# Segment mean over sorted ids: the in-kernel list planner gets measured fetch latencies, real sizes of the table work, and planned constants

## The chip, the cores and the metric

One core of one Trainium2 chip. The metric is device time in microseconds (us), the median of several executions of the one program. Engine names in the profile: DVE is VectorE, ACT is ScalarE, POOL is GpSimd, SP is SyncE, PE is TensorE.

## The reference, cut to what matters

```python
n, num_segments = 10_000_000, 10000
data        = np.random.randn(n).astype(np.float32)
segment_ids = np.sort(np.random.randint(0, num_segments, n))

sums, counts = np.zeros(num_segments, np.float32), np.zeros(num_segments, np.float32)
np.add.at(sums, segment_ids, data)
np.add.at(counts, segment_ids, 1)
return sums / np.maximum(counts, 1)
```

The ids are sorted, and a segment has about 1000 elements. The kernel never loads all ids. It lays the data out as 128 partitions by 78125 elements and cuts each partition into 90 rows of 875. A row holds at most one boundary between two segments. It finds the place of that boundary (the **cut** of the row) from a few probed ids and one short gathered run of ids.

## The kernel before

Each row costs VectorE one `split` (the sum left of the cut; rows, splits and cuts are counted from 0) and ScalarE one `total`. A cut needs a chain over four engines: SyncE loads probes, VectorE turns them into an index, GpSimd issues a gather of 175 or 208 ids for each partition, ScalarE sums the gathered ids, and VectorE makes the cut from the sum. 90 gathers share a ring of 18 buffers.

```python
def gather(odd, r, i):                                  # GpSimd
    n, idx = (WO, IDXO) if odd else (W, IDX)
    nc.gpsimd.indirect_dma_start(out=GT[:, i % RING, 0:n], ...,
        in_offset=bass.IndirectOffsetOnAxis(ap=idx[:, r : r + 1], axis=0), ...)

def add_ids(odd, r, i):                                 # ScalarE
    nc.scalar.activation(out=junk_a[:, 0:n], in_=gt32[:, i % RING, 0 : 2 * n : 2],
        func=ACT.Copy, accum_out=to[:, r : r + 1])

def split(r):                                           # VectorE, 90 times
    nc.vector.scalar_tensor_tensor(
        out=junk_v[:, 0:n], in0=iota[:, 0:n], scalar=KK[:, r : r + 1], in1=d,
        op0=ALU.is_lt, op1=ALU.mult, accum_out=A[:, r : r + 1])
```

All splits write their unused product into one buffer, `junk_v`. ScalarE does the same: every `total` and every `add_ids` writes into `junk_a`.

Nothing is scheduled at run time. While the program is built, a small simulation (class `Plan`) decides in which order each engine gets its instructions. Its idea of time is a handful of numbers:

```python
free = {"V": 4.0, "A": 6.2, "P": 3.0, "S": 0.75}        # when each engine starts
...
if moves:                                               # a load or a gather
    pipes[e].append([n, moves, now + 1.2])              # start-up, then moving
...
if pipes[e][0][1] <= 0:                                 # moved: when is it seen?
    heapq.heappush(events, (now + 1.25, len(out), pipes[e].popleft()[0]))
```

Table work (counts, prefix sums, tables of segments, checks) is tied to splits by hand: `put(r, steps, every)` hangs one or more steps behind split `r`, then behind split `r + 1`, and so on.

## Time and profile before

| | before |
|---|---|
| time | 215.02 us, median of 3 (214.88 to 215.25) |
| span of the profiled run | 212.3 us |
| busy: DVE, ACT, POOL | 142.7, 138.2, 99.6 us |
| split | 90 times, 1116 ns each |
| gather on POOL | 90 times, 1.0 us each, one per 1.3 us at best |

The lines of this profile are shown in the prediction below. No engine is busy all the time, and VectorE, the busiest, idles some 70 us. The question is what each hole of VectorE waits for.

### The profile page before, as it was taken

How to read it: one execution, taken by the hardware profiler on the slowest of the kernel's cores; microseconds unless marked ns; L12 is line 12 of the kernel's file. 1: busy time of each engine (PE TensorE's matmuls, PEld its weight loads, DVE VectorE, ACT ScalarE, POOL GpSimd, SP SyncE). 2: the span in 40 equal slices, each digit the busy share in tenths (PEclk: the TensorE clock that was granted, in tenths of full speed). 3: DMA queues.
4: the chain of work that ended last, by engine and by line, in shares of the span. 5: the costliest groups of instructions: out<-in, count | busy, mean ns of one | idle time of the engine just before them, and what ended most of it. 6: DMA issues, size and time to landing. Idle time of an engine off the chain costs nothing.

```text
span 212.3 us, 1523 instructions
## 1 busy us (share of the span) xinstructions
PE 1.6 (1%) x6; PEld 1.4 (1%) x6; DVE 142.7 (67%) x501; ACT 138.2 (65%) x362; POOL 99.6 (47%) x121
## 2 busy tenths in 40 slices
PE   0000000000000010000000000000000000010000
PEld 0000000000000010000000000000000000000000
DVE  6425083849904945974391789937927999987992
ACT  8429256546358478936883982878768997669700
POOL 5561756514773777377357147720730002883000
DMA  5999999999999999999999999999993000330000
GB/s 83 281 275 225 273 255 285 278 299 347 364 342 359 350 361 356 346 402 407 403 407 380 318 320 406 400 403 418 416 399 131 0 0 3 87 96 0 0 2 11
DMA packets 49782, 55.67 MB, mean 262 GB/s; under 512 B 39633, under 2 KB 40201, under 8 KB 49768
## 3 DMA queue, kind: packets, MB, share of 16 engines
q1 hardware_dynamic: 43835, 40.33, 59.0%
q0 software_dynamic: 5760, 15.22, 21.2%
q14 instruction: 15, 0.11, 0.2%
q10 hardware_dynamic: 172, 0.00, 0.1%
HBM read 57.81 MB, written 0.04 MB: 272 GB/s over the span
## 4 chain that ended last, share of the span: by engine, by line
issue 25%; DMA 22%; SPq 21%; DVE 15%; POOL 8%; ACT 5%; POOLq 0%; ACTq 0%; DVEq 0%
SPq L237 14%; DMA GT<-in_segment_ids_dram,IDXO 10%; POOL GT L412 8%; DVE junk_v L513 8%; DMA GT<-in_segment_ids_dram,IDX 8%; SPq L252 7%; DMA data_t<-in_data_dram 4%; ACT junk_a L508 3%; ACT junk_a L423 2%; POOLq L412 0%; DVE shf L859 0%; DVE most L932 0%; DVE pa L888 0%; DVE add L924 0%; POOL pb L890 0%
## 5 line engine op out<-in xcount | busy, mean ns | idle before, releaser
L513 DVE SCALAR_TENSOR_TENSOR junk_v<-iota,q,data_t 128x875 bf16<-128x875 f32 x90 | 100.5, 1116 | 0.8
L508 ACT ACTIVATE junk_a<-data_t 128x875 bf16<-128x875 f32 x90 | 83.6, 929 | 4.6 <-DVE FE L385 1.8
L412 POOL DMA_INDIRECT GT<-in_segment_ids_dram,IDX x49 | 49.3, 1007 | 51.6 <-DVE IDX L394 22.8
L423 ACT ACTIVATE junk_a<-GT 128x175 bf16<-128x175 int32 (+1 forms) x90 | 33.4, 372 | 56.8 <-DMA GT<-in_segment_ids_dram,IDX 32.5
L412 POOL DMA_INDIRECT GT<-in_segment_ids_dram,IDXO x41 | 41.1, 1002 | 39.1 <-DVE SR L488 14.6
L433 DVE SCALAR_TENSOR_TENSOR q<-YY,GS 128x6 f32<-128x6 f32 (+1 forms) x9 | 1.5, 166 | 34.2 <-ACT junk_a L423 34.2
L508 ACT ACTIVATION_READ_ACCUMULATOR junk_a<-data_t 128x1 f32 x90 | 16.8, 187 | 0.0
L423 ACT ACTIVATION_READ_ACCUMULATOR junk_a<-GT 128x1 f32 x90 | 16.8, 186 | 0.0
L500 DVE TENSOR_TENSOR q<-YO,GSO 128x3 f32<-128x3 f32 (+1 forms) x14 | 2.2, 160 | 21.4 <-ACT junk_a L423 21.3
L513 DVE DVE_READ_ACCUMULATOR junk_v<-iota,q,data_t 128x1 f32 x90 | 7.3, 82 | 0.0
L268 ACT ACTIVATE GT<-q 128x3744 int32<-128x3744 f32 x1 | 3.5, 3533 | 0.0
L369 DVE CAST VV<-pr 128x12 f32<-128x12 int32 (+1 forms) x9 | 1.5, 165 | 2.9 <-DMA pr<-in_segment_ids_dram 2.9
L924 POOL TENSOR_TENSOR xa<-pa,RG 128x528 f32<-128x528 f32 x1 | 1.2, 1247 | 3.6 <-DVE ps L746 3.6
L326 DVE CAST jj<-jj_i 128x128 f32<-128x128 int32 x1 | 1.5, 1485 | 0.7 <-POOL jj_i L325 0.7
L491 DVE SCALAR_TENSOR_TENSOR YO<-VV,SR 128x6 f32<-128x6 f32 (+2 forms) x9 | 1.8, 201 | 0.2
L385 DVE TENSOR_SCALAR FE<-ST 128x6 f32<-128x6 f32 (+2 forms) x10 | 1.9, 194 | 0.0
L268 ACT ACT_TABLE_LOAD x1 | 1.3, 1283 | 0.7 <-PEq L1130 0.7
L390 DVE TENSOR_TENSOR ST<-ST,FE 128x6 f32<-128x6 f32 (+2 forms) x10 | 1.6, 163 | 0.1
L394 DVE SCALAR_TENSOR_TENSOR IDX<-ST,wb 128x6 int32<-128x6 f32 (+2 forms) x11 | 1.7, 161 | 0.0
L399 DVE SCALAR_TENSOR_TENSOR YY<-ST,SG 128x6 f32<-128x6 f32 (+2 forms) x10 | 1.7, 168 | 0.0
L891 POOL TENSOR_SCALAR pb<-pb 128x168 f32<-128x168 f32 (+1 forms) x2 | 1.6, 787 | 0.2
L439 DVE TENSOR_SCALAR q<-q 128x6 f32<-128x6 f32 (+1 forms) x9 | 1.5, 169 | 0.2
(151 smaller groups left out, 61.5 us busy)
## 6 DMA issues: line engine op xcount, KB each, us to landing
data_t<-in_data_dram SPq DMA_DIRECT2D x44, 875.0 KB, 13.2
GT<-in_segment_ids_dram,IDX POOLq DMA_INDIRECT x49, 6.5
pr<-in_segment_ids_dram SPq DMA_DIRECT2D x42, 6.0 KB, 6.2
GT<-in_segment_ids_dram,IDXO POOLq DMA_INDIRECT x41, 6.8
data_t<-in_data_dram SPq DMA_DIRECT2D x1, 437.5 KB, 14.8
data_t<-in_data_dram SPq DMA_DIRECT2D x1, 125.0 KB, 14.7
out_dram<-OUT SPq DMA_DIRECT2D x1, 36.6 KB, 2.6
pt<-in_segment_ids_dram SPq DMA_DIRECT2D x2, 11.0 KB, 7.4
```

The costliest lines, as they stand in the source:

```text
L237: nc.sync.dma_start(out=pr[:, a:b, :], in_=bass.AP(ids_p.tensor, ids_p.offset + 2 * L * a, [list(ids_p.ap[0]), [2 * L, b - a], [S, K + 1]]),)
L252: nc.sync.dma_start(out=d[:, 0 : c - a], in_=data_p[:, a:c])
L268: nc.scalar.activation(out=gt32[:, :, 0 : 2 * WO : 2], in_=view(q5[:, 0, 0:1], [[0, RING], [0, WO]]), func=ACT.Copy)
L385: v.tensor_scalar(out=FE[:, a:b], in0=ST[:, a:b], scalar1=0.0, scalar2=FAR, op0=ALU.is_equal, op1=ALU.mult)
L394: v.scalar_tensor_tensor(out=IDX[:, c:d], in0=ST[:, c:d], scalar=float(w), in1=wb[:, c:d], op0=ALU.mult, op1=ALU.add)
L399: v.scalar_tensor_tensor(out=YY[:, a:b], in0=ST[:, a:b], scalar=float(K + 1), in1=SG[:, a:b], op0=ALU.mult, op1=ALU.add)
L412: nc.gpsimd.indirect_dma_start(out=GT[:, i % RING, 0:n], out_offset=None, in_=ids2d[:], in_offset=bass.IndirectOffsetOnAxis(ap=idx[:, r : ...
L423: nc.scalar.activation(out=junk_a[:, 0:n], in_=gt32[:, i % RING, 0 : 2 * n : 2], func=ACT.Copy, accum_out=to[:, r : r + 1],)
L491: nc.vector.scalar_tensor_tensor(out=YO[:, c:d], in0=VV[:, 2 * c + 1 : 2 * d : 2], scalar=float(WO), in1=SR[:, c:d], op0=ALU.mult, op1=ALU ...
L500: nc.vector.tensor_sub(out=KK[:, 2 * c + 1 : 2 * d : 2], in0=YO[:, c:d], in1=GSO[:, c:d])
L508: nc.scalar.activation(out=junk_a[:, 0:n], in_=d, func=ACT.Copy, accum_out=t)
L513: nc.vector.scalar_tensor_tensor(out=junk_v[:, 0:n], in0=iota[:, 0:n], scalar=KK[:, r : r + 1], in1=d, op0=ALU.is_lt, op1=ALU.mult, accum_ ...
```

## The change

The intent: let the planner know what a fetch really takes, so that it stops placing cuts too early; give it the true sizes of table steps and let it place them itself against deadlines; and take constants out of the start.

```diff
-        free = {"V": 4.0, "A": 6.2, "P": 3.0, "S": 0.75}
+        free = {"V": 3.4, "A": 6.2, "P": 2.2, "S": 0.75}
...
-                    heapq.heappush(events, (now + 1.25, len(out), pipes[e].popleft()[0]))
+                    heapq.heappush(events, (now + (1.4 if e == "S" else 3.8), len(out), pipes[e].popleft()[0]))
...
-    def put(r, steps, every=1, needs=()):
-        for i, f in enumerate(steps):
-            after[r + i // every].append((f, needs))
+    def put(name, by, steps, needs=(), past=()):
+        deps = list(needs) + [ends[n] for n in past or ("copy",)]
+        for i, f in enumerate(steps):
+            busy = getattr(f, "busy", 0.1)
+            plan.add((name, i), "V", busy, deps, by, f, late=busy + 0.1)
+            deps = [(name, i)]
+        ends[name] = deps[0]
...
-    put(E + 1, extend(), needs=cut_of_rows(E) + totals(E))
-    put(E + 6, ext_rows())
-    put(37, keys(0, 48), needs=[("E", 6, 0)])
+    put("ext", 40, extend() + ext_rows(), cuts(E) + rows(E) + seen(E))
+    put("keys0", 44, keys(0, 48), seen(48))
... (some 25 more such sequences)
-    nc.gpsimd.iota(rp_i[:, 0:NR], ...)                 # and 28 more constants, at once
+    for n, f in enumerate(ramps):
+        plan.add(("ramp", n), "P", 0.25, [], 5.5, f)
+    for n, f in enumerate(copies):
+        small(("copy", n), [...], 2.2, f)
... (probes of later rows asked for 27 instead of 31 rows ahead; the last seven rows' ids
     loaded row by row; one rule of the choice between split and small work, and 0.1 us more for a split right
     after a split)
```

## The prediction

> **What bounds the kernel now.** I read the view of cores first (one core, span 212.3 us, clock 1.000, so no throttling), then the busy slices of the page, the stretches of the span with each engine's busy time, the waits, and the order in time of VectorE (DVE) and GpSimd (POOL) around the long waits. The slices come first, because they show when the transfers stop:
>
> ```profile
> DVE  6425083849904945974391789937927999987992
> ACT  8429256546358478936883982878768997669700
> POOL 5561756514773777377357147720730002883000
> DMA  5999999999999999999999999999993000330000
> ```
>
> A slice is 5.3 us. The DMA row is full from the second slice to the 30th and then falls, so the bulk of the data has been fetched by about 163 us. DVE is the other way round: full of holes before that point, and nearly solid after it. The stretches put numbers on it (width, then busy time of PE, PEld, DVE, ACT, POOL with counts, clock, DMA share, GB/s):
>
> ```profile
> 18.78:60.00 41.22, 0.00 (x0) 0.00 (x0) 27.16 (x109) 20.97 (x64) 22.80 (x23) 1.00 1.08 287
> 60.00:107.00 47.00, 0.98 (x4) 0.93 (x4) 26.13 (x88) 34.09 (x103) 29.08 (x30) 1.00 1.05 372
> 107.00:163.40 56.40, 0.00 (x0) 0.00 (x0) 39.40 (x129) 41.15 (x113) 26.11 (x26) 1.00 0.99 370
> 163.40:208.30 44.90, 0.59 (x2) 0.50 (x2) 42.51 (x133) 31.26 (x70) 12.21 (x15) 1.00 0.08 22
> ```
>
> While data arrives DVE idles 14.1, 20.9 and 17.0 us; afterwards it works off 45 us of backlog with 2.4 us idle. The end is therefore set by DVE: 142.7 us of its own work, plus its holes, plus 4.0 us for the output. The view of waits names the holes:
>
> ```profile
> DVE q L433 <- ACT junk_a L423: 34.2, 9, 7.3
> DVE q L500 <- ACT junk_a L423: 21.3, 6, 5.6
> DVE VV L369 <- DMA pr<-in_segment_ids_dram: 2.9, 1, 2.9
> DVE q L449 <- ACT junk_a L423: 1.9, 2, 1.2
> ```
>
> L433, L500 and L449 turn sums of gathered ids into the cut position of a row. 57.4 us go to them: DVE reached the cut before its gathers had landed and been summed by ACT, and because its program is one fixed order, rows that were ready behind the cut stood still. The timeline of DVE shows the longest such place. This cut's six indices were written at 49.10, but on POOL its last gather started only at 59.15, behind others; DVE has nothing placed before the cut but index work that ends at 58.8:
>
> ```profile
> 58.56 0.17 DVE L394 SCALAR_TENSOR_TENSOR IDX<-ST,wb 128x6 int32<-128x6 f32 x1
> 66.05 0.17 DVE L433 SCALAR_TENSOR_TENSOR q<-YY,GS 128x6 f32<-128x6 f32 x1 [7.25 <-ACT junk_a L423]
> ```
>
> The DMA issues say why: a gather needs 6.5 to 6.8 us from issue to landing, while the planner of before counts 1.2 us to start, 0.40 or 0.47 us of moving, and 1.25 us to land.
>
> ```profile
> GT<-in_segment_ids_dram,IDX POOLq DMA_INDIRECT x49, 6.5
> GT<-in_segment_ids_dram,IDXO POOLq DMA_INDIRECT x41, 6.8
> ```
>
> **What the Trainium skill says.** "PSUM — Partial Sum Buffer", Engine vs sequencer instructions: ScalarE, VectorE and GpSimd queues are strictly first in, first out. The 7.25 us hole agrees. "Perfetto Trace Analysis", DMA Instruction — SWDGE (GPSIMD): the profiled end of a gather is the end of descriptor writing, not of the movement. It agrees: POOL shows 1.00 us per gather, issue to landing is 6.5. "DMA: Bandwidth & Descriptors", Anatomy of one DMA — SWDGE (gpsimd) path: 2.0 us fixed plus bytes at 436 GB/s. A gather of 128x175 ids of 8 bytes is 179 KB, so 2.4 us as an estimate from that page; the trace has 3.0 us only for the last seven gathers, issued after the data had stopped, and 5 to 8.5 us under load, so the measured time is what I use.
>
> **The change, part by part.** No arithmetic is dropped; the change re-sorts the same work. (1) The planner's landing time of a gather goes from 1.25 to 3.8 us (with 1.2 and 0.4: 5.4 us plus sharing), of a data or probe load to 1.4. In the built program the order moves accordingly. In before, the gathers of even and odd cuts alternate on POOL, and an odd one not yet computable holds up the even ones behind it: POOL stood still 14.6 us on SR and 8.9 us on IDXO. In after, all three even gathers of the second group go ahead of the first odd one. On DVE, the first six-row even cut (the one of the 7.25 us) has 12 splits, 5 to 16, between its indices and itself, where before it had 6; the next such cut has 11. (2) The table work becomes sequences with real sizes and a deadline; the sizes of the instructions stay. (3) Fourteen constants leave DVE's start-up and fill holes; ident's fill moves to POOL. (4) The last seven rows' ids are fetched row by row, and their indices come before split 69, where before they came before split 72; in before POOL sat idle 22.8 us and then cost DVE only 1.9 us, so this is small.
>
> Value of (3): DVE's first probe work waits for its fetch at 6.7 us either way, and the first cut needs gathers issued at 8.7, 10.2 and 11.5 plus about 5.7 us landing and 0.6 us of ACT, thus 18 us in both. The 2 us of constants fall into holes: 0 to 0.5 us at the end. The gain must come from (1).
>
> **Working of the new waits.** I walk the new order with durations of the old trace: 1.17 us from split to split (49.88, 51.05, 52.23 in the timeline), 0.08 to 0.12 us for a small operation, the listed duration for bigger ones, 1.3 us from gather to gather on POOL (1.00 busy, 0.30 gap), landing 5.5 us up to 45 us, 6.6 up to 90, 7.3 later and 8.2 near 140 (what the gathers of before took in those stretches), and 0.6 us for ACT's sum and the signal. Each cut starts at the later of DVE reaching it and its last gather being summed. The start-up idle up to the first split stays at 11 us. From there:
> - First odd cut: its two gathers can be issued at 20.3 and 21.6, ready 27.7; DVE has nothing else and waits 4.8. The next three cuts wait 0.3, 1.6, 0.9.
> - Split 16 ends at 52 us (before: 56.8). The fourth odd cut: gathers 47.0 to 49.6, ready 56.9, reached 53.5: 3.4.
> - Up to split 28 the cuts have slack: the fifth even group is ready at 73 and reached at 75.
> - From 77 to 98 us POOL runs without gap, and the cuts follow its beat: waits of 0.7, 1.2, 1.5, 1.9 and 3.2 us (the last for six gathers ending at 98.3, ready 106.3, reached 103.1). Split 44 ends near 108; in before it is near 127.
> - After that 0.3, 1.2, 2.5 and 1.3 us, and about 0.8 us for the matmul behind the verdict, which now has little work beside it. Split 77 ends near 163.5.
> These are 25.6 us; with the 11 at the start, the 2.5 us that before has beyond its named waits (65.6 idle to 208.3, 63.1 named), and perhaps 1 us for the last total, 40 us of idle. DVE's end is 142.7 + 40 = 183; the output adds 4.0, the span is 187. The measured median of before is 2.7 us over its profiled span (215.0 against 212.3), so the time is 189 to 190; I take **189 us**, 12% less.
>
> Data does not stop this: the transfers have the same bytes and end near 160. Split 77 needs the 39th of 45 tiles; at a pace of some 2.2 us a tile that lands near 149, and it is used at 163. The ring of 18 tiles also stops blocking: at split 44 near 108 us, 40 tiles may be issued.
>
> **The rivals.** *Floor by transfers.* If the waits vanish more fully than in my walk, the last tile decides: landing at 160 to 163, two splits, and 5 us to the end, plus some 5 us of table work after split 87. That gives a span of 172 and a time of 175. For it: DMA was full all along; against: POOL's 90 gathers at 1.3 us are 117 us by themselves, and the first odd cuts chain two gathers one after the other. *Latency grows with the load.* In before the sync queue stood blocked for a free tile (one load 15.25 us in the DMA queue's timeline), which thinned the traffic. A faster DVE frees tiles sooner, so gathers would meet a full queue from 60 us on: 8.2 instead of 7 us each, seen at 130 to 150 us. Some ten tight cuts by about 1 us: 199. *A fixed order with a wrong model still waits.* Only positions moved, and ACT is in order too: a sum of ids behind a total whose tile is late holds a cut. If half of the 57 us survive at other cuts, the time is 200 to 205. *Nothing gained*, since the holes only move to the tail: against it stands that the tail is solid work on DVE, so every earlier split shortens it.
>
> **Range and chances.** The walk gives 189; about 175 is the floor; latency under load gives up to 199. I put 80% on 180 to 199. For a gain under 2% (above 210.7) more than 50 of the 57 us would have to return; slower needs new waits. Chances: faster 0.97, same 0.02, slower 0.01.
>
> **What would show it right or wrong.** Right: DVE busy stays within 1.5 us of 142.7; waits of DVE on ACT's id sums fall from 57 us to between 22 and 32; DMA still ends near 160; split 44 ends near 108, and the stretch after the data stops shrinks from 45 to about 21 us, still solid. The start to the first split stays near 19 us. Wrong on the first step, if DVE's waits stay above 40 us; on the floor, if DVE begins to wait for data tiles near the end; on the latency, if gathers have a median above 8 us; on the constants, if the first split comes before 17 us.

## The result, and the profile after

The changed kernel took **200.89 us** (median of 4, 200.19 to 202.13), the kernel before in the same rounds 215.13 us. The ratio is 0.9345, 95% interval 0.9296 to 0.9395. Ratios here are the mean time of one kernel's runs over that of the other's runs of the same rounds, so they are not quite the ratio of the quoted medians. Executions over 1.5% slower than the fastest of the same kernel are left out of the means. It is a gain of 6.5% where 12% was predicted: right in direction, 12 us short, and just outside the range.

The slices of the page, as in the prediction, now 5.0 us each:

```profile
DVE  6225475549939851599559717989979978999990
POOL 8537777751457777017777401767406958402000
DMA  5999999999999999999999999999999824200000
```

DVE is fuller from the middle on, but thin slices remain at 35 to 45 us (8th and 9th) and at 70 to 85 us (15th to 17th). The stretches, in the columns of the prediction:

```profile
18.78:60.00 41.22, 0.00 (x0) 0.00 (x0) 24.67 (x92) 25.13 (x77) 24.65 (x25) 1.00 1.10 302
60.00:107.00 47.00, 0.99 (x4) 0.93 (x4) 33.08 (x123) 31.08 (x89) 29.18 (x30) 1.00 1.06 358
107.00:163.40 56.40, 0.00 (x0) 0.00 (x0) 45.07 (x137) 44.71 (x116) 27.32 (x30) 1.00 0.98 372
163.40:197.00 33.60, 0.58 (x2) 0.50 (x2) 31.18 (x92) 24.57 (x60) 8.30 (x8) 1.00 0.12 31
```

DVE's work before 163.4 us grew, and the backlog after it shrank from 45 to about 33 us; the prediction had 21. The first stretch (18.78 to 60) got worse: 16.6 us idle instead of 14.1. The view of waits of the changed kernel, its longest rows (total, times, longest; "..." marks a row left out):

```profile
DVE VV L389 <- DMA pr<-in_segment_ids_dram: 12.4, 4, 5.6
DVE q L520 <- ACT junk_a L443: 8.1, 6, 3.3
DVE q L453 <- ACT junk_a L443: 6.6, 2, 5.3
DVE junk_v L533 <- remote: 5.8, 3, 2.5
DVE q L520 <- issue: 4.7, 4, 2.0
DVE PX L818 <- issue: 3.7, 1, 3.7
...
DVE junk_v L533 <- issue: 1.7, 1, 1.7
```

The cuts (L453 and L520) now wait 19.4 us where they waited 57: this part worked even better than predicted. But other rows grew. VectorE waits for probes (L389) for 14.5 us (this row and one of 2.1 us that is left out), where it was 2.9 before; some 9 us of this lie before the first split, which starts at 17.3 us, not later than the 18.8 of before. And, which is new, it waits before splits (L533) and table steps (L818) for "remote" or "issue", that is, for nothing that the profile can name. Its timeline shows what these are. Before splits:

```profile
36.94 1.13 DVE L533 SCALAR_TENSOR_TENSOR junk_v<-iota,q,data_t 128x875 bf16<-128x875 f32 x1 [0.76 <-DVE YY L419]
...
39.76 1.13 DVE L533 SCALAR_TENSOR_TENSOR junk_v<-iota,q,data_t 128x875 bf16<-128x875 f32 x1 [1.68 <-remote]
...
42.59 1.13 DVE L533 SCALAR_TENSOR_TENSOR junk_v<-iota,q,data_t 128x875 bf16<-128x875 f32 x1 [1.70 <-issue]
```

and before table steps:

```profile
77.12 0.18 DVE L653 TENSOR_TENSOR delta<-sp,base 128x1 f32<-128x1 f32 x1
81.01 0.26 DVE L818 TENSOR_TENSOR_SCAN PX<-bpx,PX 128x20 f32<-128x20 f32 x1 [3.70 <-issue]
82.43 0.19 DVE L657 TENSOR_SCALAR NBP<-q 128x48 f32<-128x48 f32 x1 [1.16 <-DVE PX L818]
```

In the built program the last two of these splits (39.76 and 42.59) and L818 wait for VectorE's own semaphore alone. A split waits until the split before it has signalled that `junk_v` may be written again; L818 reads what L812 wrote, and L812 had ended 2.1 us before the stand began. So the work was done, and VectorE stood still until its own signal had come back. These stands (holes of over 0.4 us before an instruction that is neither a cut nor waits for a load or for another engine) come to 5.8 us between 36 and 46 us and 8.7 us between 71 and 82 us, 15.4 us in the whole kernel. In the kernel before there are none. The prediction has no term for them.

Two more things mark the same stretches. The trace lacks most records of semaphore changes there: 8 to 14 per 5 us from 25 to 45 us, where the trace of before has 124 to 141. And 26 of the 90 gathers took 9.3 to 13.7 us from their start on GpSimd to the start of their sum on ScalarE; in the trace of before none took over 8.7. The transfers were not slower: by the packets of the gather queue (64 for each gather, taken in order), the last data of these 26 had arrived 3.5 to 6.2 us after the start. (The trace of before records landings too; there this reckoning falls 0.2 to 1.8 us before each.) The other 3.6 to 7.8 us passed before ScalarE began the sum, because ScalarE stood too:

```profile
77.47 0.94 ACT L528 ACTIVATE junk_a<-data_t 128x875 bf16<-128x875 f32 x1 [1.68 <-remote]
...
80.30 0.36 ACT L443 ACTIVATE junk_a<-GT 128x175 bf16<-128x175 int32 x1 [1.80 <-issue]
...
82.40 0.94 ACT L528 ACTIVATE junk_a<-data_t 128x875 bf16<-128x875 f32 x1 [1.65 <-remote]
```

ScalarE's waits for the data and ids of these three had gone through before; what was left to wait for was ScalarE's own semaphore, which guards `junk_a`. Ten such holes of over 0.4 us come to 15.0 us; in the kernel before there are none. The gathers behind them then queue on ScalarE. So signals came late on two engines. The runs below were made with VectorE's in view; none of them takes the wait from ScalarE.

GpSimd issues gathers there with hardly a pause, from 17.6 to 43.7 us and from 56.7 to 80 us:

```profile
65.87 1.00 POOL L432 DMA_INDIRECT GT<-in_segment_ids_dram,IDX  x1 [0.30 <-issue]
67.17 1.00 POOL L432 DMA_INDIRECT GT<-in_segment_ids_dram,IDX  x1 [0.30 <-issue]
```

The walk of the prediction reaches the cut of the fifth even group (counted from 0) at 75 us; in the trace it is reached at 87.0, and split 28 behind it ends at 88.9. From this cut to the end of the span the walk has 112 us and the trace 113. So nearly all of the miss is made before split 28.

### The profile page after: what moved, and what is told of

Read it like the earlier page. It is cut to its first block, busy times and chain, and to the rows that moved or that the text cites. A ratio compares the mean times of both kernels' runs of the same rounds, so it can differ in the third digit from the quotient of the medians.

```text
span 200.3 us, 1521 instructions
## 1 busy us (share of the span) xinstructions
PE 1.6 (1%) x6; PEld 1.4 (1%) x6; DVE 142.6 (71%) x500; ACT 138.3 (69%) x362; POOL 101.1 (50%) x122
## 4 chain that ended last, share of the span: by engine, by line
DVE 38%; DMA 21%; issue 18%; SPq 7%; ACT 6%; another core or an unknown queue 5%; POOL 2%; POOLq 0%; DVEq 0%; ACTq 0%
DVE junk_v L533 25%; DMA GT<-in_segment_ids_dram,IDXO 11%; SPq L244 4%; DMA data_t<-in_data_dram 4%; DMA pr<-in_segment_ids_dram 3%; DMA GT<-in_segment_ids_dram,IDX 3%; SPq L259 3%; ACT junk_a L443 3%; ACT junk_a L528 3%; POOL GT L432 2%; DVE PX L818 1%; DVE q L474 1%; DVE YY L419 1%; DVE q L520 1%
## 5 line engine op out<-in xcount | busy, mean ns | idle before, releaser
L533 DVE SCALAR_TENSOR_TENSOR junk_v<-iota,q,data_t 128x875 bf16<-128x875 f32 x90 | 100.8, 1120 | 10.1 <-remote 5.8
L528 ACT ACTIVATE junk_a<-data_t 128x875 bf16<-128x875 f32 x90 | 83.6, 929 | 17.5 <-DMA data_t<-in_data_dram 5.5
L432 POOL DMA_INDIRECT GT<-in_segment_ids_dram,IDXO x41 | 42.5, 1036 | 47.2 <-DVE IDXO L503 14.9
L389 DVE CAST VV<-pr 128x12 f32<-128x12 int32 (+1 forms) x9 | 1.7, 191 | 14.5 <-DMA pr<-in_segment_ids_dram 12.4
L520 DVE TENSOR_TENSOR q<-YO,GSO 128x3 f32<-128x3 f32 (+1 forms) x14 | 2.3, 161 | 12.9 <-ACT junk_a L443 8.1
L533 DVE DVE_READ_ACCUMULATOR junk_v<-iota,q,data_t 128x1 f32 x90 | 7.4, 82 | 0.0
L453 DVE SCALAR_TENSOR_TENSOR q<-YY,GS 128x6 f32<-128x6 f32 (+1 forms) x9 | 1.5, 163 | 6.6 <-ACT junk_a L443 6.6
L818 DVE TENSOR_TENSOR_SCAN PX<-bpx,PX 128x20 f32<-128x20 f32 x1 | 0.3, 260 | 3.7 <-issue 3.7
L459 DVE TENSOR_SCALAR q<-q 128x6 f32<-128x6 f32 (+1 forms) x9 | 2.1, 231 | 0.1
```

The costliest lines, as they stand in the source:

```text
L432: nc.gpsimd.indirect_dma_start(out=GT[:, i % RING, 0:n], out_offset=None, in_=ids2d[:], in_offset=bass.IndirectOffsetOnAxis(ap=idx[:, r : ...
L459: nc.vector.tensor_scalar(out=rows_of(a, b), in0=rows_of(a, b), scalar1=MID, scalar2=None, op0=ALU.min)
L520: nc.vector.tensor_sub(out=KK[:, 2 * c + 1 : 2 * d : 2], in0=YO[:, c:d], in1=GSO[:, c:d])
L528: nc.scalar.activation(out=junk_a[:, 0:n], in_=d, func=ACT.Copy, accum_out=t)
L533: nc.vector.scalar_tensor_tensor(out=junk_v[:, 0:n], in0=iota[:, 0:n], scalar=KK[:, r : r + 1], in1=d, op0=ALU.is_lt, op1=ALU.mult, accum_ ...
L818: v.tensor_tensor_scan(out=PX[:, 1 : E + 1], data0=bp, data1=bp, initial=PX[:, 0:1], op0=ALU.max, op1=ALU.max)
```

## The experiments

**Theory A:** VectorE's own signals come late in dense runs of gathers, and it is this that ate the missing gain. **Rival B:** the engine stands for another reason, and the wait is only what happens to be written beside it. **Rival C:** the new table order or the constants cost what is missing. First come runs that take the change apart.

### The changed kernel again

No edit.

> The changed kernel once more, unaltered, for a second trace. In its first trace VectorE stood still for 8.7 us between 71.5 and 82.5 us, and 5.7 us between 36 and 46 us, before instructions whose only wait is on VectorE's own semaphore, and in the same stretches most records of semaphore updates are missing. Theory A (the miss is these standstills and they belong to the kernel): they come back at the same instructions, with the same widths to 1 us, and the time is 200 to 202. Theory B (they are a disturbance of that one execution): they are gone or elsewhere in the second trace, and split 28 ends at 78 to 82 us instead of 88.9; then the time of the undisturbed execution should be near 192, or, if it stays at 200, waits of another kind must stand in their place.

Measured: 200.69 us (199.73 to 201.2); the kernel before in these rounds 214.61; ratio 0.9337. VectorE stood 13.1 us on its own signals, 8.0 us of it between 71 and 82 us (the same table steps, one more step and a split) and 5.1 us before splits between 36 and 44 us. The stands repeat; they are no accident of one execution.

### The changed kernel with the old landing number

```diff
-   heapq.heappush(events, (now + (1.4 if e == "S" else 3.8), ...
+   heapq.heappush(events, (now + 1.25, ...
```

> The changed kernel with the one number undone: the planner counts 1.25 us for the landing of gathers and loads again, everything else stays. If the measured landing time is what brings the gain (my step 1), the waits of VectorE on ACT's id sums return to 45 to 60 us and the time to 208 to 216. If the gain comes from the table work as sequences with deadlines and from the other planner numbers, it stays at 199 to 204.

Measured: 212.47 us (211.35 to 212.65), ratio 0.9884. The waits on id sums are back (51 us before L453 and L520), and of the stands on own signals one of 0.6 us is left. ScalarE has no stand either. Without the landing number, the whole rest of the change is worth 2 us.

### The kernel before with the new landing number alone

> The kernel before with that one number changed alone: 3.8 us for gathers, 1.4 us for loads. If my step 1 holds and works by itself, the waits on id sums fall to below 35 us and the time to 198 to 205. If the planner needs the real sizes and deadlines to use it, the time stays above 207.

The edit is the reverse of the last one, in the kernel before. Measured: **197.04 us** (196.11 to 197.5), ratio 0.9173. One number gives 17.6 us, and it beats the whole change by 3.7 us. Its waits:

```profile
DVE q L500 <- ACT junk_a L423: 18.1, 6, 6.6
DVE q L433 <- ACT junk_a L423: 5.9, 2, 5.5
...
DVE junk_v L513 <- DVE junk_v L513: 2.2, 3, 1.0
```

The cuts wait 27.7 us here (these two rows and 3.7 us put down to "issue"), 8 us more than in the changed kernel, but the stands on own signals are 6.9 us instead of 13 to 15. The rest of the change bought shorter cut waits and paid for them with stands. That fits A, but does not show it.

### Constants first

```diff
-    for n, f in enumerate(ramps): plan.add(("ramp", n), "P", 0.25, [], 5.5, f)
-    for n, f in enumerate(copies): small(("copy", n), [...], 2.2, f)
+    for f in ramps + copies: f()
+    small(("copy", len(copies) - 1), [], 2.2, lambda: None)
```

> The changed kernel with its fills, ramps and copies written at the start of the program, ahead of the planned part, as before. My step (3) says they lie in holes either way: within 1 us of the changed kernel, 199.5 to 202. The rival, that the earlier first index and gather (first gather at 6.8 us instead of 8.7) carry through to the end, says 2 us slower, 202 to 204.

Measured: 200.41 us, ratio 0.9344; the changed kernel in the same rounds had 0.9337. So the place of the constants in the program is worth nothing measurable, and rival C is out for it. The second half of the expectation is not tested: the first gather went out at 6.6 us in this run and at 6.8 us in the changed kernel, against 8.7 us before, so the earlier start was not undone.

### Four buffers for the unused product

This is the test between A and B: a split no longer has to wait for the split just before it, and nothing else changes.

```diff
-    junk_v = cpool.tile([P, L], BF16, name="junk_v")
+    junk_v = [cpool.tile([P, L], BF16, name=f"junk_v{i}") for i in range(4)]
...
-            out=junk_v[:, 0:n], in0=iota[:, 0:n], ...
+            out=junk_v[r % 4][:, 0:n], in0=iota[:, 0:n], ...
```

> The changed kernel with one thing altered: the splits write their unused product into four buffers in turn, so that a split no longer waits for the semaphore of the split just before it. Order and work are the same. In the changed kernel VectorE stood 5.8 us before four splits between 36 and 46 us and 8.7 us between 71 and 82 us (one split, the rest table steps), though the instruction waited for was long over. Theory A (VectorE's own signals come late there): the stands before splits at 36 to 46 us fall to under 1 us in all, the stands before table steps stay, split 16 ends near 50 us instead of 54.7, and the time falls by 1 to 5 us, to 196 to 200. Rival B (the engine stands for another reason, such as fetching instructions, and the wait is only what happens to be written beside it): the stands stay at the same splits at over 4 us in all, and the time is 200 to 201.5.

Measured: **197.21 us** (196.43 to 197.52), ratio 0.9223. The same splits of the same stretch:

```profile
37.81 1.13 DVE L533 SCALAR_TENSOR_TENSOR junk_v<-iota,q,data_t 128x875 bf16<-128x875 f32 x1
...
38.85 1.13 DVE L533 SCALAR_TENSOR_TENSOR junk_v<-iota,q,data_t 128x875 bf16<-128x875 f32 x1
...
39.90 1.13 DVE L533 SCALAR_TENSOR_TENSOR junk_v<-iota,q,data_t 128x875 bf16<-128x875 f32 x1
```

Splits that had started 2.8 us apart follow each other by 1.05 us. One stand of 1.9 us is left before them, at a split that waits for a small instruction just before it. Split 16 ends at 50.0 instead of 54.8 us. The stands before table steps, whose dependences are real, stay at 8 us. So before splits the engine was not halted: it stood on the signal. B falls there. By the ratios, which allow for the other rounds, the gain is 2.4 us, by the medians 3.5. (My expectation of under 1 us left was a little too good.)

### Table steps kept apart

```diff
-            plan.add((name, i), "V", busy, deps, by, f, late=busy + 0.1)
+            plan.add((name, i), "V", busy, deps, by, f, late=busy + 2.0)
```

> The changed kernel with one number altered in the planner: a table step counts as done 2.0 us after its work instead of 0.1, so that the planner puts a split between two steps of which one needs the other. Theory A (late own signals cost what is placed back to back): the stands of VectorE before table steps at 71 to 82 us (8.7 us in the changed kernel) fall under 3 us, split 28 ends near 83 us instead of 88.9, and the time falls by 3 to 7 us, to 194 to 198. Rival C (the late signals were hidden time, and the cuts behind it take it over): waits on id sums rise by what the stands fall, and the time is 199 to 202. Rival D (table work put between the splits delays them, which is how the kernel before lost time): split 44 ends later than 122.7 us and the time is above 201.

Measured: **196.97 us** (195.78 to 197.39), ratio 0.9199. The planner now puts splits between steps of which one needs the other. The stands at 71 to 82 us fall from 8.0 to 5.0 us (one of 4.0 us moved to a split, which still shares one buffer), and split 28 ends at 83.6 us. My bound of 3 us was missed, the gain was as expected (3.7 us by the medians, 3.0 by the ratios), and C and D of the expectation do not appear: split 44 ends at 115.0 us instead of 122.7.

### Probe loads with a measured landing too

```diff
-   (now + (1.4 if e == "S" else 3.8), len(out), pipes[e].popleft()[0])
+   n = pipes[e].popleft()[0]
+   (now + (1.4 if n[0] == "data" else 3.8), len(out), n)
```

> The changed kernel with the landing of a probe load also set to what was measured (3.8 us instead of 1.4, as for gathers; the probes took 6.2 us from issue to landing in the kernel before). In the changed kernel VectorE waited 14.5 us on probes before 34 us, in the kernel with only the landing number changed 10.4 us. If these waits are a loss of their own, the wrong latency of probes is a second reason why the change fell short: waits on probes fall under 9 us, split 8 ends near 40 us instead of 43.5 and the time is 196 to 199. If they lie in holes that the first gathers leave anyway, the waits move to the cuts, split 8 stays at 42 to 44 us and the time is 199.5 to 202.

Inconclusive: 193.32 us once, 198.61 to 200.51 us three times. In the profiled run (a slow one) waits on probes fell from about 13 to 5 us and split 8 ended at 39.8 us, as the first theory said, but at split 26 (84.4 us) the gain was lost again, with 10 us of stands before table steps. As this is a slow run, it explains nothing.

### Landing number and four buffers, without the rest of the change

> The kernel before with the new landing number alone (197.0 us) and, besides, four buffers for the unused product of the splits. That kernel stood 7 us on VectorE's own signals, 5 us of them before splits between 60 and 71 us. Theory A (late own signals): the stands before splits vanish, and the time falls by 1 to 4 us, to 193 to 196, below both kernels of the case. Rival B (the engine stands for another reason): the stands stay and the time is 196.5 to 197.5.

The edits of two runs above together, in the kernel before. Measured: 195.78 us (195.26 to 197.08), ratio 0.9144. No stand before a split is left, and 2.3 us before table steps. The gain over the landing number alone is only 1.3 us by the medians and 0.6 by the ratios (0.9173 there, in other rounds), within the noise: what the splits no longer stood, the next cuts waited (33 us instead of 27.7). A cut that is late anyway hides a stand. ScalarE, whose sums the cuts need, still stood 10.2 us on its own signals.

### Both shelters

The buffers and the steps apart together, in the changed kernel.

> The changed kernel with both: four buffers for the unused product of the splits (alone 197.21 us) and table steps counted as done 2.0 us later by the planner (alone 196.97 us). If each took away its own part of VectorE's stands on its own late signals (some 5.8 us before splits, 8.7 us before table steps in the changed kernel), the two add up: the stands fall under 3 us in all and the time is 192 to 195, below everything so far. If what either gains is given back at the same next cut (a hole hidden behind another), the time is 195.5 to 197.5.

Measured: **193.93 us** (193.38 to 194.94), ratio 0.9058, the best of all. The two add up: 3.5 and 3.7 us alone, 6.8 us together (against 200.69; by the ratios 2.4, 3.0 and 6.0 us). The changed order of tables is now better than the old one with the same buffers (195.78), so it was not the order that cost, but the way it was packed. My bound on the stands was wrong again: 9.7 us of them remain, in fewer and other places (4.7 us before one step of a cut at 40 us), and as many on ScalarE.

### With the probes' landing as well

> The one before in this job with the landing of the probe loads at 3.8 us in the planner as well, which alone gave 193.3 us once and 198.6 to 200.5 us three times. If the spread of that run came from VectorE's late own signals, it closes here to under 2 us and the time is 190.5 to 194. If the wrong latency of probes is worth nothing, the time equals that of the run before within 1 us. If the spread stays over 4 us, it comes from something else.

Measured: 198.92 us (197.62 to 199.6), ratio 0.9307, a clear loss against the run before. The front gained what was hoped: split 28 ends at 78.4 us and split 44 at 108.0, 4.3 us ahead of the last run. But in the built order the index work of the last seven rows now stands before split 67 instead of before split 60, and VectorE waited 7.9 us at three late cuts between 158 and 169 us. The spread is 2 us, so the spread of the single run above is not settled by this.

### Gathers paced

What makes the signals late? The fill below touches nothing that anybody reads.

```diff
+        if 12 <= i < 30 or 36 <= i < 51:           # after the gathers of the two long runs
+            nc.gpsimd.memset(pace, 0.0)            # 128 x 476 f32, 0.5 us
```

> The changed kernel with 0.5 us of idle work on GpSimd (a fill of a scratch tile) after each of the 33 gathers of the two long unbroken runs, so that a gather is issued each 1.8 us instead of 1.3; all else the same. It asks what makes the signals late. If it is the dense run of gathers, the stretches in which semaphore records are missing (25 to 45 and 60 to 80 us) fill again, VectorE's stands there fall from 14 us to under 4, and what the slower pace costs the cuts (some 8 us a run) is about paid for: 197 to 203. If the pace has nothing to do with it, the records stay missing, the stands stay over 8 us, and the time rises to 203 to 212.

Measured: **197.04 us** (196.3 to 197.47), ratio 0.9186: *slower* gathers made the kernel faster by 3.7 us. GpSimd:

```profile
66.91 1.00 POOL L433 DMA_INDIRECT GT<-in_segment_ids_dram,IDX  x1 [0.16 <-issue]
67.91 0.51 POOL L442 MEMSET pace<- 128x476 f32 x1
```

A gather each 1.67 us instead of 1.3. Not one stand of over 0.4 us on own signals is left in the whole kernel, on VectorE or on ScalarE. The cuts wait 30.7 us now, so most of what the stands gave back went there. The same table steps that took from 76.84 to 82.43 above:

```profile
72.38 0.55 DVE L650 TENSOR_SCALAR KEY<-VV,base 128x48 f32<-128x48 f32 x1
...
72.63 0.30 DVE L656 TENSOR_TENSOR delta<-sp,base 128x1 f32<-128x1 f32 x1
72.70 0.25 DVE L821 TENSOR_TENSOR_SCAN PX<-bpx,PX 128x20 f32<-128x20 f32 x1
72.97 0.53 DVE L660 TENSOR_SCALAR NBP<-q 128x48 f32<-128x48 f32 x1
```

(The numbers of lines are 3 higher because of the edit: L821 here is L818 above.) The same order, the same dependences, 0.6 us instead of 5.6. The records of semaphore changes come back in the paced stretches (18, 43, 82, 110 per 5 us from 25 to 45 us) and stay missing from 100 to 110 us (19 and 13), where nothing is paced. The gathers of the two runs reach their sums after 4.5 to 7.4 us again. So the dense runs of gathers are what brings the late signals of this order: slow the gathers, and they are gone. The pace alone does not decide, though. In the kernel before 14 gathers follow each other by 1.3 us (67.1 to 85.0 us), in this run 13 (92.4 to 109.0 us), both without a stand; the second run of the changed kernel has 18, and VectorE's first stand there begins when 12 have started. What else it takes was not tested.

### The kernel before with four buffers

> The kernel before with nothing changed but four buffers for the unused product of the splits. It is the control for the gain that these gave the changed kernel (3.5 us). In the kernel before VectorE hardly stands on its own signals, so if those are the cause, the buffers are worth nothing here: 213.5 to 215.5 us, within 0.5% of the kernel before. If the wait of each split on the last one costs time always, 90 splits gain here too: 209 to 212.

The control came out between the two expectations: 212.27 us (210.82 to 213.79), ratio 0.9905, interval 0.984 to 0.997. Four buffers are worth about 1.8 us even without stands. In a quiet stretch a split that waits for the last one follows by 1.17 us (the prediction's timeline), without the wait by 1.05. So a good part of what the buffers gave the changed kernel is this steady 0.12 us a split. By the ratios they gave 2.4 us there and 2.0 us here, with intervals of 0.5 to 1.4 us on either side, so the times do not show how much the late signals cost; that the splits no longer stand is shown by the trace alone. The table steps' gain has no such control, and its edit also changes the order. The records of semaphore changes also thin out in places of this run (10 to 29 per 5 us at 55 to 65 and 75 to 85 us) without any stand, so missing records alone prove nothing.

### Pacing and both shelters

> Four buffers and table steps apart (193.93 us) and, besides, the 0.5 us fill on GpSimd after each of the 33 gathers of the long runs. Theory (dense runs of gathers make signals late, the other two edits only shelter VectorE from it): with the signals on time the last stands (4.7 us before L459 at 40 us, 4.9 us before table steps at 71 to 78 us) go, waits on the cuts change little, and the time is 189 to 193. If the shelter had already taken the gain, the slower gathers only cost: 194 to 197.

Measured: 196.72 us (196.16 to 197.13), ratio 0.9174; the second expectation, against the theory. No stand is left, but the cuts wait 34 us where the run without pacing had 21. Once VectorE is sheltered, dense gathers are worth more than punctual signals in this kernel.

### Half the pace

The same fill with 170 elements; it took 0.26 us, so that a gather starts each 1.42 us.

> The changed kernel with a shorter fill after the same 33 gathers (170 instead of 476 elements, some 0.2 us, which may vanish in the 0.3 us that lie between two gathers anyway). It asks for the dose. If the mere instruction between the gathers helps, the stands of VectorE between 36 and 46 and between 70 and 82 us are gone as with the long fill, and the time is near 197. If it is the rate (a gather each 1.67 us instead of 1.3), the short fill leaves most of the late signals, the stands stay over 8 us, and the time is 199 to 201.

Measured: 196.97 us (196.55 to 198.27), ratio 0.9173. The stands stay, though milder: 11.0 us, none over 1.9 us, and the records stay missing (14 to 17 per 5 us from 25 to 45 us). The gathers' time to their sums falls to 9.4 us at most. So the rate counts, not the mere presence of another instruction. The time was better than my 199 to 201. VectorE's stands do not explain that; ScalarE's fell from 13.7 us (in the run again) to 5.3, and the cuts wait 20 us, as in the changed kernel.

### Pacing to the end

```diff
-        if 12 <= i < 30 or 36 <= i < 51:
+        if 12 <= i < 67:
```

> The changed kernel with the 0.5 us fill after all gathers from the 12th to the 66th, so that the third stretch of missing records (95 to 115 us), which the first paced run left alone, is paced as well. If dense gathers are the trigger there too, the records of 100 to 115 us return (over 40 per 5 us instead of 13 to 19), the 12th to 17th cut no longer find sums late, and the time is 193 to 196.5. If the slower pace costs more there than it gives, since the cuts follow GpSimd's beat there, 197 to 200.

Measured: 201.09 us, ratio 0.9374. The records are back (77 and 100 per 5 us from 100 to 110 us, nowhere under 33 before 150 us), no stand is left, and no gather takes over 7.3 us to its sum. Yet the time is that of the changed kernel, because the cuts follow GpSimd's beat:

```profile
DVE q L456 <- ACT junk_a L446: 17.0, 5, 6.8
...
DVE q L523 <- ACT junk_a L446: 13.4, 10, 3.7
```

With the 3.3 us put down to "issue", 34 us of cut waits stand against 19 in the changed kernel. In these runs pacing trades punctual signals for later gathers.

### Steps apart and paced, one buffer

> Table steps apart and paced gathers, with the one buffer of the changed kernel. If the late signals are the only reason why four buffers help, they are worth nothing here: the time is within 1 us of the same kernel with four buffers, and no stand before a split is longer than 0.6 us. If the buffers help otherwise, it is 2 us or more slower than that one.

Measured: 198.28 us, ratio 0.9233, against 0.9174 with four buffers: 1.6 us. It lies between the two expectations and agrees with the 1.8 us of the control: with signals on time the buffers give about the steady 0.12 us a split. No stand before a split is longer than 0.3 us.

The main runs in short (stands: sum of the engine's holes of over 0.4 us on its own signals):

| kernel | us | VectorE's stands, us | ScalarE's stands, us | split 28 ends at |
|---|---|---|---|---|
| before | 215.0 | 0 | 0 | 89.5 |
| before + landing number | 197.0 | 6.9 | 11.3 | 84.3 |
| before + landing number + buffers | 195.8 | 2.3 | 10.2 | 83.9 |
| changed (run again) | 200.7 | 13.1 | 13.7 | 88.3 |
| changed + buffers | 197.2 | 10.4 | 7.7 | 85.2 |
| changed + steps apart | 197.0 | 10.5 | 10.6 | 83.6 |
| changed + both | 193.9 | 9.7 | 9.7 | 81.4 |
| changed + paced | 197.0 | 0 | 0 | 80.5 |
| changed + both + paced | 196.7 | 0 | 0 | 80.7 |

## Why the prediction was right or wrong

**Right: where the gain comes from.** The landing number is the change's only large part. With it taken out 12 us are lost, and alone it gives 17.6 us. VectorE's waits on id sums fell from 57 to 19 us, below the 22 to 32 foreseen. (A stand before a cut shortens the wait at it; with slower gathers and no stands the cuts wait 30.7 us.) DVE's busy time (142.6 us), the first split (18.4 us) and the end of the transfers (about 160 us) came as predicted.

**Right in size, for a wrong reason: the constants.** Their place in the program is worth nothing measurable. But the probes were not awaited until "6.7 us either way": in the trace of before VectorE only came to them then (idle 0.01 us), after its constants, and in the changed kernel it read them at 4.8. The first gathers went out 1.9 us earlier, the first split ended 1.5 us earlier, and what that is worth was not tested. (The diff moves fifteen constants of VectorE besides ident, not fourteen.)

**Wrong: the step "Up to split 28 the cuts have slack".** The walk let VectorE wait at cuts alone and gave ScalarE 0.6 us from a gather's landing to its sum and signal. Both failed. In the dense runs of gathers that the new order makes, VectorE stood 13 to 15 us on its own signals, for which the walk has no term, and ScalarE 14 to 15 us, so that 26 sums began 3.6 to 7.8 us after the last data. The data themselves came on time. Split 28 ended 12 us late. The balance agrees: up to its end (195.8 us) VectorE idled 53 us where the walk has 40, and its waits at cuts and probes after the first split were 24.5 us, where the walk has 25.6 of named waits; the stands of 15.4 us are what was left out. The link to the gathers is shown by the slower ones, which remove the stands on both engines with the order unchanged. Two shelters that leave the gathers alone give back 6.8 us, to 193.9. The last 5 us to 189 were not recovered; that version still has 9.7 us of stands on VectorE and 9.7 on ScalarE, whose one buffer no run changed, and which of these holds the 5 us is not shown.

**Wrong: part (2) as neutral.** "The sizes of the instructions stay" is true, but the planner held a table step for done after 0.1 us and packed dependent steps back to back, where the old code had put a split between most of them. With steps apart 3.7 us came back (3.0 by the ratios).

**The rivals.** "Latency grows with the load" had the right size (199) by luck. The last data of a gather came 5.75 us after its start in the median, against 5.95 before; what grew was ScalarE's delay. "A fixed order with a wrong model still waits" had the right number (200 to 205), also by luck, as the waits did not move to other cuts. A sum of ids held up on ScalarE, which it names, did occur, but behind late signals and not behind a late tile.

**Two readings in the walk** were a little off without weight for the result. The 2.7 us from the span to the time compare a median with another execution; the profiled one itself took 214.11 us, 1.8 over its span. And gathers under load landed after 3.8 to 8.5 us in the trace of before, not 5 to 8.5.

**Open.** Whether the signal itself travels late or an engine is late to act on it; whether it is the rate of gathers, the length of their run or the number in flight that counts (at 7 us each, 1.3 us apart, some five are, by estimate); how much ScalarE's stands cost, since no run gave it more buffers; and whether taking the trace adds to the stands, since no run tells a traced execution from an untraced one and records go missing in the same stretches. Also the two-valued times of the run with measured probes (193.3 and 199 to 200.5 us).

## What to carry to other kernels

When a planner or a hand-made order is given true fetch latencies, give it the latency of an engine's own signals too: dependent small steps and a shared scratch output cost little as long as signals return at once (0.12 us a split here), and microseconds when they do not (up to 4.7 us here). Look at every engine that shares a scratch output, not only at the busiest. Rotate scratch outputs that nobody reads, put independent work between dependent steps, and test a suspected late signal by removing what the instruction waits for. And a fast source can be too fast: slowing 33 gathers by 0.4 us each removed every stand, which is a cheap way to find such a cause even where it is not the best cure.

## What the Trainium skill lacked or had wrong

- "Perfetto Trace Analysis", DVE / Act Engine Instruction (TENSOR_ADD, Activation, etc): it puts the propagation of an instruction's semaphore update after the end that the profiler reports, without a size. Here waiting for it cost 0.12 us from split to split in quiet stretches (1.17 against 1.05 us), and up to 3.7 us before one table step and 2.4 us before one sum on ScalarE in dense runs of gathers.
- "DMA: Bandwidth & Descriptors", Anatomy of one DMA — SWDGE (gpsimd) path: its fixed cost plus bytes gives 2.4 us for such a gather (an estimate from that page). In the kernel before the gathers took 6.5 to 6.8 us in the median under load, and 3.0 us after the data had stopped. That long runs of gathers 1.3 us apart can come with late signals of other engines, and runs 1.67 us apart did not, stands nowhere that I found.
- No page that I found says when records of semaphore changes are missing from a trace like these (8 to 14 per 5 us in such stretches, where the trace of before has over 120), so that waits are put down to "remote" or "issue". What the pages say of record queues that are full is general, and no run here tells whether a full one held an engine up.
